# Two-layer decoder trunk on one core: GpSimd's two-operand steps given to VectorE, sigmoids computed by Tanh

## The chip, the core and the metric

One core of a Trainium2 chip runs the whole program. The metric is device microseconds of one execution. TensorE is PE in the profile, VectorE DVE, ScalarE ACT, GpSimd POOL, and SyncE SP, which only issues DMAs.

## The reference, cut to what matters

x is 1024 tokens by 1024 channels, mem 256 memory vectors. Each layer norms x, projects it, mixes it over time, adds a memory attention of 4 heads, gates with SiLU and projects back. Layer 0 mixes with 12 heads of causal attention whose queries and keys are built from normed low-rank projections and partly rotated; layer 1 with the recurrence of RWKV-7.

```python
for i in range(DEPTH):
    h, m = rmsnorm(x, norm_g[i]), rmsnorm(mem, mem_norm_g[i])
    mem_k, mem_v = split_cols(m @ w_mem_kv[i], (X_WIDTH, X_WIDTH))
    u = h @ (w_in_mla[0] if i == 0 else w_in_rwkv[0])
    # layer 1, of the columns of u:
    w = -jax.nn.softplus(-(w0 + jnp.tanh(wd) @ w2)) - 0.5
    decay = jnp.exp(-jnp.exp(w))
    a = jax.nn.sigmoid(a0 + ad @ a2)
    y = jnp.concatenate([mix, mem_out], axis=-1) * jax.nn.silu(gate)
    x = x + y @ w_out[i]
return rmsnorm(x, final_g)
```

The kernel computes exp(-exp(w)) as exp(-C0 * sigmoid(w0 + ...)) with C0 = exp(-0.5), and silu(gate) in layer 1 as gate * sigmoid(gate).

## The kernel before, in words

All matrices are kept transposed, channels on the 128 partitions and tokens along the row, in two halves (`hf`) of 512 tokens.

**Products by halves.** A product in fp32 is made of three in fp32r: each operand is split into a high half (ScalarE rounds it, `copy`) and a low half (the operand minus its high half). `mm3` (L162 to L164) issues high by high, low by high and high by low. `weights` (L142) does this for a weight tile of 128x512: a DMA into `wr`, ScalarE's cast to `wh` (L153), a subtraction to `wl` (L155). In layer 0 the subtraction is GpSimd's, with every second tile of the memory's weights (`shared`) on VectorE; `layer1` sets `lows`, and from there on all are VectorE's. `wr`, `wh` and `wl` have four buffers each, and a projection of 128 channels (`gemm`, 24 matmuls of 512 columns) uses two tiles. Two PSUM tiles (`mm`) take the products in turn.

**Norms.** `rstd` is a chain over three engines. ScalarE squares the tiles, VectorE adds them up (L186), TensorE sums over partitions (L208), VectorE takes an inverse square root by Newton steps on 8 elements per partition (L194 to L199) and widens it (L213), TensorE spreads it (L220), ScalarE copies it out (L222).

**Layer 0.** The opening loads x, splits it (`load_x`, L440 and L441), projects the first six blocks for both halves (`low`), norms them (`lora`), rotates the shared key (`rope`, whose second product L523 is GpSimd's), norms and splits the memory (`mem_load`, `mem_norm`: scale L255, halves L128 and L129) and projects it (`mem_kv`). Then come gates and memory heads, then attention, where each pair of heads is projected while earlier heads attend. There GpSimd makes the low halves of the rotated queries (L640, L641) and fills the masked corner of a tile with zeros (L730). The output projection follows.

**Layer 1.** 24 items (12 pairs of heads by 2 halves) pass through five stages that run side by side: `project`, `prep` (the decay and a by two sigmoids, L998, then exponentials, L1037 to L1040), `invert`, `scan`, `norm`. Gates (`gate`, L864) and memory heads (with the softmax exponential, L304) are strewn in. ScalarE evaluates a function from the table that is loaded; where the next function needs another, an ACT_TABLE_LOAD stands before it. Sigmoid and Exp are in different tables.

**What sets the order.** The code gives the program, but a scheduler reorders each engine's instructions when the program is built, by its own estimates of their durations and by the buffers. On the chip each engine takes its instructions strictly in that order, and so does SP's queue of DMAs. Moving a step to another engine thus moves others as well.

Of the kernel before, what the change touches and what calls it, by code (L numbers as in the profile page):

```python
# [13 lines left out]
F32 = mybir.dt.float32  # L14
# [3 lines left out]
AF = mybir.ActivationFunctionType  # L18
# [38 lines left out]
PNG, PMG, PFG, PQG, PKVG, PMU, PW0 = 0, 16, 32, 40, 43, 45, 82  # L57
# [14 lines left out]
class Build:  # L72
    def __init__(self, tc, A, st):
        self.tc, self.nc, self.A = tc, tc.nc, A
        self.n, self.lows = 0, False
        pool = lambda name, bufs, **kw: st.enter_context(tc.tile_pool(name=name, bufs=bufs, **kw))
        self.const = pool("const", 1)
        self.wp = pool("w", 4)
        self.w2p = pool("w2", 1)
        self.ws = pool("ws", 4)  # L80
        self.smp = pool("sm", 4)
        self.heap = pool("heap", 54)
        self.heap2 = pool("heap2", 12)
        self.mmp = pool("mmp", 2, space=PSUM)
        self.dram = pool("dram", 1, space=DRAM)
        self.ysp = [None, None]
        dt = lambda s: self.dram.tile([P, T], F32, tag=s, name=s)
        self.mkd = [[dt(f"mk{l}{i}") for i in range(2)] for l in range(2)]
        self.mvd = [[dt(f"mv{l}{i}") for i in range(2)] for l in range(2)]
        self.carry = [self.dram.tile([P, P], F32, tag=f"cr{p}", name=f"cr{p}") for p in range(NH)]  # L90
        self.setup()
# [31 lines left out]
        return self.prm[:, i : i + 1]  # L123


    def split(self, hi, lo, src):

        self.nc.scalar.copy(hi, src)  # L128
        self.nc.vector.tensor_sub(lo, src, hi.bitcast(F32))  # L129
# [9 lines left out]
        self.split(hi[:], lo[:], src)  # L139
        return hi, lo  # L140

    def weights(self, src, cols=1024, shared=False):  # L142


        nc = self.nc
        res = []
        for c in range(0, cols, T):
            n = min(T, cols - c)
            raw = self.wp.tile([P, T], F32, tag="wr", name=self.name("wr"))
            hi = self.ws.tile([P, T], F32R, tag="wh", name=self.name("wh"))  # L150
            lo = self.ws.tile([P, T], F32R, tag="wl", name=self.name("wl"))
            nc.sync.dma_start(raw[:, :n], src[:, c : c + n])
            nc.scalar.copy(hi[:, :n], raw[:, :n])  # L153
            sub = nc.vector.tensor_sub if self.lows or shared and len(res) % 2 else nc.gpsimd.tensor_sub
            sub(lo[:, :n], raw[:, :n], hi[:, :n].bitcast(F32))  # L155
            res.append((hi, lo))
        return res

# [104 lines left out]
    def mem_kv(self, l, ms):  # L263

        nc, A = self.nc, self.A
        mk, mv = [], []
        for h in range(4):
            if h % 2 == 0:
                mk.append(self.g([P, 2, 256], s="mk"))
            w = self.weights(A["wmk"][l, h], shared=True)  # L270
            ps = self.mmt()
            self.gemm(ps[:, :256], w, ms, 8)
            nc.scalar.copy(mk[-1][:, h % 2, :], ps[:, :256])
        for cb in range(2):
            ws = self.weights(A["wmv"][l, cb, 0], shared=True) + self.weights(A["wmv"][l, cb, 1], shared=True)
            ps = self.mmt()
            for mb in range(2):
                for k in range(8):
                    hi, lo = ws[k // 2]
                    o = (k % 2) * 256  # L280
                    m = tuple(x[:, mb * P : mb * P + P] for x in ms[k])
                    self.mm3(
                        ps[:, mb * 256 : mb * 256 + 256], m, (hi[:, o : o + 256], lo[:, o : o + 256]), k == 0, k == 7
                    )
            t = self.g(s="mv")
            nc.scalar.copy(t[:], ps[:])
            mv.append(t)
        for i, t in enumerate(mk):
            nc.sync.dma_start(self.mkd[l][i][:].rearrange("p (h m) -> p h m", h=2), t[:])
        for i, t in enumerate(mv):  # L290
            nc.sync.dma_start(self.mvd[l][i][:], t[:])
# [122 lines left out]
    def layer0(self, ahead):  # L414

        nc, A, tc = self.nc, self.A, self.tc
        with ExitStack() as st:
# [5 lines left out]
            b_tile = lambda: psb.tile([P, T], F32, tag="b", name=self.name("b"))  # L423
# [40 lines left out]
            raw = [[None] * 6 for _ in range(2)]  # L464
# [27 lines left out]
            cos, sin = tl([P, S], F32, "cos"), tl([P, S], F32, "sin")  # L492
# [23 lines left out]
            def rope(q, hf):  # L516

                sl = slice(hf * T, hf * T + T)
                sw, t = self.g(s="rs"), self.g(s="rt")
                for b in range(4):  # L520
                    nc.sync.dma_start(sw[32 * b : 32 * b + 32, :], q[32 * (b ^ 1) : 32 * (b ^ 1) + 32, :])
                nc.vector.tensor_mul(t[:], q[:], cos[:, sl])
                nc.gpsimd.tensor_mul(sw[:], sw[:], sin[:, sl])  # L523
                nc.vector.tensor_add(t[:], t[:], sw[:])
                return t

# [81 lines left out]
            def project(h):  # L608
# [26 lines left out]
                for t in rot:  # L635

                    a, b = self.g(dt=F32R, s="qsa"), self.g(dt=F32R, s="qsb")
                    nc.scalar.copy(a[0:64, :], t[0:64, :])
                    nc.scalar.copy(b[64:128, :], t[64:128, :])
                    nc.gpsimd.tensor_sub(a[64:128, :], t[0:64, :], a[0:64, :].bitcast(F32))  # L640
                    nc.gpsimd.tensor_sub(b[0:64, :], t[64:128, :], b[64:128, :].bitcast(F32))  # L641
                    hd["qr"].append(a)
                    heads[h + 1]["qr"].append(b)
                if h % 2 == 0:
# [134 lines left out]
    def layer1(self, x1, first, second):  # L779

        nc, A, tc = self.nc, self.A, self.tc
        with ExitStack() as st:
# [17 lines left out]
            nc.gpsimd.memset(rmask[:].rearrange("p (c t) -> p c t", t=64)[:, :, 0:1], 0.0)  # L800
            prev = tl([P, 37], F32, "prev")

            cen = tl([P, P], F32, "cen")
            nc.vector.scalar_tensor_tensor(cen[:], self.bones, -1.0 / 64, self.ident, ALU.mult, ALU.add)
            ARs = [tl([P, 8, 256], F32, f"AR{i}") for i in range(3)]
# [4 lines left out]

            self.ysp[1] = [[self.dram.tile([P, T], F32, tag=f"y1_{k}_{hf}", name=f"y1_{k}_{hf}") for hf in range(2)] for k in range(16)]
            am = self.cst[:, CAM : CAM + 256]
            env = dict(rmask=rmask, cen=cen, am=am, ip=ip, a_tile=a_tile, b_tile=b_tile, c_tile=c_tile, y_tile=y_tile)
            xns, twa = [None, None], [tl([P, T], F32R, f"twa{i}") for i in range(2)]
            items = [dict(AR=ARs[i % 3], XT=XTs[i % 2], U2=U2, p=i % NH, hf=i // NH, twa=twa) for i in range(2 * NH)]

# [44 lines left out]
            def gate(m, hf, tile=self.mmt):  # L861
                ps = proj(41 + m, hf, tile)
                sg = self.g(s="sg")
                nc.scalar.activation(sg[:], ps[:], AF.Sigmoid)  # L864
                nc.vector.tensor_mul(sg[:], ps[:], sg[:])
                return sg

# [70 lines left out]
                    next(gen, None)  # L938
                    yield

            self.lows = True
            N, now = 2 * NH, [0]
            stages = [(project, ST[0]), (lambda i: self.prep(items[i], env), ST[1]), (lambda i: self.invert(items[i], env), ST[2]), (scan, ST[3]), (norm, ST[4])]
            extra = {}
# [34 lines left out]
    def prep(self, d, env):  # L979
# [14 lines left out]
        for j, (t, bias) in enumerate(((sig, PW0), (a, PA0))):  # L994
            ps = a_tile()
            mm(ps[:], wh[:, j * P : j * P + P], twa[j][:], start=True, stop=False)
            mm(ps[:], wl[:, j * P : j * P + P], twa[j][:], start=False, stop=True)
            ACT.activation(t[:], ps[:], AF.Sigmoid, bias=self.pc(bias + p))  # L998

        yield  # L1000

# [377 lines left out]
```

## Time and profile before

| | us |
|---|---|
| three runs, median (lowest, highest) | 2541.62 (2540.92, 2550.03) |
| the profiled execution | 2544.33 |
| its span in the profile | 2542.6 |
| TensorE busy | 2434.1 |
| VectorE busy | 1883.6 |
| ScalarE busy | 1371.9 |
| GpSimd busy | 285.0 |

The span runs from the first to the last instruction; the rest of the execution's time lies around it. TensorE's busy time is no measure of its speed, since matmuls overlap and run at either of two clocks: 2.4 GHz, or half of it; PEclk is the mean share of the full clock in a stretch. Layer 0 takes the time up to about 1045 us.

### The profile page before, as it was taken

The numbers are of one execution on the slowest core, as the hardware profiler recorded it, in microseconds if no ns is written. First come the engines' busy times: TensorE is split into PE (matmuls) and PEld (weight loads), VectorE is DVE, ScalarE is ACT, GpSimd is POOL, SyncE is SP. The second block draws the span as 40 slices with busy tenths as digits, with TensorE's granted clock in tenths as the row PEclk, the third lists the DMA queues.
The fourth block names the chain that finished last, engine by engine and source line by source line (L and its number), as shares of the span: only waits on it lengthen the run. The fifth ranks groups of instructions, "written<-read, shape, count | busy, mean of one in ns | idle before, by whom it ended". The sixth has DMA issues, their size and how long they took to land.

```text
span 2542.6 us, 39928 instructions
## 1 busy us (share of the span) xinstructions
PE 2434.1 (96%) x13298; PEld 2003.9 (79%) x13298; DVE 1883.6 (74%) x5564; ACT 1371.9 (54%) x2971; POOL 285.0 (11%) x344
## 2 busy tenths in 40 slices
PE   7899999999999999999999999999999999999997
PEld 5688777888888787878777777877787777788885
DVE  6655433677777647679888888788888888786986
ACT  5444335555445434556566665666666665654542
POOL 3332222322222240000000000000000000000000
PEclk8899999999999999999999999999999999999998
DMA  4242222111111345331222222322222223232341
GB/s 155 88 157 96 91 83 80 50 50 60 55 54 56 135 140 178 122 106 61 80 67 70 74 83 82 120 76 76 69 78 74 75 80 102 92 105 97 115 141 69
DMA packets 165983, 231.46 MB, mean 91 GB/s; under 512 B 46096, under 2 KB 67984, under 8 KB 165776
## 3 DMA queue, kind: packets, MB, share of 16 engines
q1 hardware_dynamic: 165776, 228.90, 27.5%
q8 instruction: 105, 1.72, 0.3%
q14 instruction: 102, 0.84, 0.1%
HBM read 187.66 MB, written 37.49 MB: 89 GB/s over the span
## 4 chain that ended last, share of the span: by engine, by line
PE 69%; DVE 16%; ACT 6%; issue 3%; DMA 2%; SPq 0%; DVEq 0%; POOL 0%; ACTq 0%; POOLq 0%
PE mm L162 14%; PE mm L163 13%; PE mm L164 13%; PE a L1088 3%; DVE tmp L1139 2%; PE c L1221 2%; PE pt L726 2%; DVE U L1143 2%; PE c L1224 1%; PE po L162 1%; PE y L1228 1%; PE po L163 1%; DVE wl L155 1%; PE y L1227 1%; PE po L164 1%
## 5 line engine op out<-in xcount | busy, mean ns | idle before, releaser
L153 ACT CAST wh<-wr 128x512 fp32r<-128x512 f32 (+3 forms) x500 | 298.6, 599 | 461.6 <-PE mm L163 363.0
L162 PE MATMUL mm<-xnh,wh 128*128 128x512 f32 x912 | 374.1, 411 | 0.8 <-DVE qml L134 0.6
L163 PE MATMUL mm<-xnl,wh 128*128 128x512 f32 x912 | 371.4, 407 | 0.0
L164 PE MATMUL mm<-xnh,wl 128*128 128x512 f32 x912 | 369.8, 406 | 0.0
L155 DVE TENSOR_TENSOR wl<-wr,wh 128x512 fp32r<-128x512 f32 (+2 forms) x352 | 237.2, 676 | 98.7 <-ACT wh L153 79.8
L155 POOL TENSOR_TENSOR wl<-wr,wh 128x512 fp32r<-128x512 f32 (+1 forms) x148 | 186.3, 1263 | 579.4 <-ACT wh L153 446.0
L162 PE MATMUL mm<-yh,wh 128*128 128x512 f32 x492 | 199.8, 406 | 5.5 <-DVE xr L391 5.3
L164 PE MATMUL mm<-yh,wl 128*128 128x512 f32 x492 | 197.6, 402 | 0.0
L162 PEld LDWEIGHTS mm<-xnh,wh 128*128 128x128 f32 x912 | 172.2, 189 | 30.4 <-issue 2.6
L163 PE MATMUL mm<-yl,wh 128*128 128x512 f32 x492 | 196.1, 399 | 0.0
L163 PEld LDWEIGHTS mm<-xnl,wh 128*128 128x128 f32 x912 | 172.4, 189 | 27.2 <-issue 1.4
L164 PEld LDWEIGHTS mm<-xnh,wl 128*128 128x128 f32 x912 | 172.2, 189 | 27.2 <-issue 1.0
L1069 POOL MEMSET SAV<- 64x512 f32 x48 | 24.9, 524 | 1385.6 <-DVE m L1261 250.7
L162 PE MATMUL mm<-xh,wh 128*128 128x512 f32 x416 | 168.9, 406 | 7.2 <-ACT xh L440 7.2
L163 PE MATMUL mm<-xl,wh 128*128 128x512 f32 x416 | 168.6, 405 | 2.9 <-DVE xl L441 2.9
L164 PE MATMUL mm<-xh,wl 128*128 128x512 f32 x416 | 168.1, 404 | 0.0
L1139 DVE TENSOR_TENSOR tmp<-As,U 128x60 f32<-128x60 f32 (+24 forms) x744 | 156.8, 211 | 13.2 <-DMA U<-in_cst_dram 1.1
L1143 DVE TENSOR_TENSOR U<-U,tmp 128x60 f32<-128x60 f32 (+24 forms) x744 | 157.2, 211 | 11.9
L1235 ACT ACTIVATE sc<-S,f 128x128 f32<-128x128 f32 x168 | 67.4, 401 | 170.0 <-DVE S L1236 155.5
L304 ACT ACTIVATE p<-b,sm 128x512 f32<-128x512 f32 (+2 forms) x144 | 82.9, 579 | 117.2 <-DVE sm L301 78.0
L391 DVE TENSOR_TENSOR xr<-mm,xr 128x512 f32<-128x512 f32 x123 | 84.5, 689 | 77.7 <-PE mm L164 77.2
L162 PEld LDWEIGHTS mm<-yh,wh 128*128 128x128 f32 x492 | 93.1, 189 | 24.3 <-DVE xr L391 3.5
(362 smaller groups left out, 6214.3 us busy)
## 6 DMA issues: line engine op xcount, KB each, us to landing
wr<-in_wu_dram SPq DMA_DIRECT2D x292, 256.0 KB, 2.6
wr<-in_wo_dram SPq DMA_DIRECT2D x122, 256.0 KB, 2.6
yr<-y SPq DMA_DIRECT2D x60, 256.0 KB, 3.7
As<-sysd SPq DMA_DIRECT2D x24, 512.0 KB, 4.3
y<-y SPq DMA_DIRECT2D x32, 256.0 KB, 2.0
y<-sg SPq DMA_DIRECT2D x32, 256.0 KB, 2.0
g<-u SPq DMA_DIRECT2D x24, 256.0 KB, 2.4
gt<-g SPq DMA_DIRECT2D x24, 256.0 KB, 2.8
```

The source lines that it names most:

```text
L153: nc.scalar.copy(hi[:, :n], raw[:, :n])
L155: sub(lo[:, :n], raw[:, :n], hi[:, :n].bitcast(F32))
L162: mm(ps, a[0], b[0], start=start, stop=False)
L163: mm(ps, a[0], b[1], start=False, stop=False)
L164: mm(ps, a[1], b[0], start=False, stop=stop)
L304: nc.scalar.activation(p[:, :own], ps[:, :own], AF.Exp, bias=sm[:, 0:1], accum_out=sm[:, 2 + i : 3 + i])
L391: nc.vector.tensor_add(xs[m][:], ps[:], xs[m][:])
L726: nc.tensor.transpose(pt[:, o : o + P], src, self.ident)
L1088: mm(ps[:, j * 256 : j * 256 + 256], BK[c // 4][:, c % 4, :], AR[:, c, :], start=True, stop=True)
L1139: E.tensor_tensor(out=tmp[:, 0:u, 0:n], in0=As[:, 0:u, u : u + 1].broadcast_to([P, u, n]), in1=U[:, u : u + 1, i0:8].broadcast_to([P, u, n ...
L1143: E.tensor_tensor(out=U[:, 0:u, i0:8], in0=U[:, 0:u, i0:8], in1=tmp[:, 0:u, 0:n], op=ALU.add)
L1235: ACT.activation(sc[:], cur, AF.Copy, scale=fc)
```

## The change

`weights` no longer chooses: every subtraction is VectorE's. The second product of `rope` and the low halves of the rotated queries go to VectorE too. GpSimd keeps the fills (`memset`, `affine_select`). In layer 1 each Sigmoid becomes a Tanh of half the argument and a Copy with scale 0.5 and bias 0.5, in place; the biases of `prep` are halved once, at the layer's setup. Only 24 columns of parameters are scaled for that.

```diff
+    def sigmoid(self, out, src, bias=None):
+        ACT = self.nc.scalar
+        ACT.activation(out, src, AF.Tanh, scale=0.5, bias=0.0 if bias is None else bias)
+        ACT.activation(out, out, AF.Copy, scale=0.5, bias=0.5)
...
-    def weights(self, src, cols=1024, shared=False):
+    def weights(self, src, cols=1024):
...
-            sub = nc.vector.tensor_sub if self.lows or shared and len(res) % 2 else nc.gpsimd.tensor_sub
-            sub(lo[:, :n], raw[:, :n], hi[:, :n].bitcast(F32))
+            nc.vector.tensor_sub(lo[:, :n], raw[:, :n], hi[:, :n].bitcast(F32))
...
-                nc.gpsimd.tensor_mul(sw[:], sw[:], sin[:, sl])
+                nc.vector.tensor_mul(sw[:], sw[:], sin[:, sl])
...
-                    nc.gpsimd.tensor_sub(a[64:128, :], t[0:64, :], a[0:64, :].bitcast(F32))
-                    nc.gpsimd.tensor_sub(b[0:64, :], t[64:128, :], b[64:128, :].bitcast(F32))
+                    nc.vector.tensor_sub(a[64:128, :], t[0:64, :], a[0:64, :].bitcast(F32))
+                    nc.vector.tensor_sub(b[0:64, :], t[64:128, :], b[64:128, :].bitcast(F32))
...
+            half = self.prm[:, PW0 : PW0 + 24]
+            nc.vector.tensor_scalar_mul(half, half, 0.5)
...
-                nc.scalar.activation(sg[:], ps[:], AF.Sigmoid)
+                self.sigmoid(sg[:], ps[:])
...
-            ACT.activation(t[:], ps[:], AF.Sigmoid, bias=self.pc(bias + p))
+            self.sigmoid(t[:], ps[:], env["half"][:, bias - PW0 + p : bias - PW0 + p + 1])
```

The built order moves in two places of the opening. The lines of the changed kernel stand 4 or 5 further down (L212 is its L208, L224 its L220). On TensorE, around the sum of squares of the memory (`b_207`); `mm_234`, `mm_236`, `mm_244` and `mm_246` are four projections in this order, before first:

```order
L163 MATMUL mm_236_1157<-xl_90_513,wh_232_1125 128x512
L164 MATMUL mm_236_1157<-xh_89_512,wl_233_1126 128x512
L208 MATMUL b_207_1045<-cst_101,sqa_199_1022 128x2 x2
L162 MATMUL mm_236_1157<-xh_92_519,wh_232_1125 128x512
L163 MATMUL mm_236_1157<-xl_93_520,wh_232_1125 128x512
...
L163 MATMUL mm_244_1200<-xl_18_238,wh_239_1189 128x512
L220 MATMUL b_210_1063<-cst_101,rw_209_1061 128x128 x2
L164 MATMUL mm_244_1200<-xh_17_237,wl_240_1190 128x512
```

and of the change, down to the first matmuls that need the memory's tiles (`mh_213`, `ml_214`):

```order
L167 MATMUL mm_246_1227<-xl_65_412,wh_239_1189 128x512
L168 MATMUL mm_246_1227<-xh_64_411,wl_240_1190 128x512
L212 MATMUL b_207_1045<-cst_101,sqa_199_1022 128x2 x2
...
L224 MATMUL b_210_1063<-cst_101,rw_209_1061 128x128 x2
L168 MATMUL mm_246_1227<-xh_103_566,wl_243_1196 128x512
L166 MATMUL mm_246_1227<-xh_106_573,wh_242_1195 128x512
L167 MATMUL mm_246_1227<-xl_107_574,wh_242_1195 128x512
L168 MATMUL mm_246_1227<-xh_106_573,wl_243_1196 128x512
L166 MATMUL mm_255_1271<-mh_213_1071,wh_250_1260 128x256
L166 MATMUL mm_262_1309<-mh_213_1071,wh_257_1298 128x256
```

The sum now comes 39 matmuls later, with the rest of `mm_236`, all of `mm_244` and a quarter of `mm_246` ahead of it, and only four matmuls stand between the spread and the memory's first product, where 43 stood. On VectorE, around the end of the first half's squares (`sqa_31`) and the start of its square root (`n_40`), before:

```order
L186 TENSOR_TENSOR sqa_31_265<-sqa_31_265,sqb_37_282 128x512
L186 TENSOR_TENSOR sqa_31_265<-sqa_31_265,sqb_38_285 128x512
L210 TENSOR_SCALAR n_40_294<-b_39_289 128x8
L194 TENSOR_SCALAR n_40_294<-n_40_294 128x8
L195 TENSOR_SCALAR n_40_294<-n_40_294 128x8
```

and now:

```order
L190 TENSOR_TENSOR sqa_31_265<-sqa_31_265,sqb_37_282 128x512
L159 TENSOR_TENSOR wl_72_426<-wr_70_424,wh_71_425 128x512
L190 TENSOR_TENSOR sqa_31_265<-sqa_31_265,sqb_38_285 128x512
L159 TENSOR_TENSOR wl_83_474<-wr_81_472,wh_82_473 128x512
L214 TENSOR_SCALAR n_40_294<-b_39_289 128x8
L159 TENSOR_TENSOR wl_86_480<-wr_84_478,wh_85_479 128x512
L198 TENSOR_SCALAR n_40_294<-n_40_294 128x8
L199 TENSOR_SCALAR n_40_294<-n_40_294 128x8
```

Three low halves of weights, which were GpSimd's, now stand inside the chain of the norm.

## Rows read from the trace of the kernel before

**Rows 1.** The page's first part: each engine's busy us, share of the span, instructions.

```profile
span 2542.6 us, 39928 instructions
...
PE 2434.1 (96%) x13298; PEld 2003.9 (79%) x13298; DVE 1883.6 (74%) x5564; ACT 1371.9 (54%) x2971; POOL 285.0 (11%) x344
```

**Rows 2.** Table of stretches: us; PE, PEld, DVE, ACT, POOL busy (instructions); PEclk; DMA; GB/s.

```profile
0.00:160.00 160.00, 128.47 (x572) 103.70 (x573) 104.88 (x186) 72.58 (x129) 51.33 (x42) 0.91 0.37 123
...
500.00:860.00 360.00, 356.16 (x2269) 308.81 (x2268) 269.17 (x646) 186.84 (x469) 77.12 (x140) 1.00 0.18 57
...
1045.00:2500.00 1455.00, 1413.32 (x7804) 1149.29 (x7803) 1220.16 (x4164) 875.57 (x1911) 23.90 (x46) 1.00 0.27 87
```

**Rows 3.** Who TensorE waited for, 0 to 160 us: total us, times, longest us.

```profile
PE b L208 <- DVE sqa L186: 13.2, 4, 4.5
...
PE b L220 <- DVE rw L213: 4.3, 2, 3.1
...
PE mm L163 <- POOL wl L155: 1.1, 1, 1.1
```

**Rows 4.** Table of stretches again: after a wait, and the opening; PEclk before DMA share.

```profile
57.00:62.00 5.00, 4.83 (x15) 4.19 (x16) 2.13 (x13) 0.96 (x2) 0.27 (x1) 0.50 0.03 13
...
20.00:140.00 120.00, 102.44 (x426) 82.64 (x427) 82.63 (x156) 52.35 (x95) 37.58 (x26) 0.89 0.29 97
```

**Rows 5.** VectorE's groups, 0 to 160 us: busy us, mean ns, idle before.

```profile
L186 DVE TENSOR_TENSOR sqa<-sqa,sqb 128x512 f32<-128x512 f32 x17 | 18.1, 1063 | 1.1 <-ACT sqb L185 0.4
L441 DVE SCALAR_TENSOR_TENSOR xl<-x,prm,xh 128x512 fp32r<-128x512 f32 x16 | 15.9, 1024 | 7.4 <-ACT xh L440 7.4
L474 DVE TENSOR_TENSOR c<-c,rx 128x512 f32<-128x512 f32 x12 | 13.5, 1134 | 8.4 <-ACT c L473 4.8 <-ACT rx L222 3.6
```

**Rows 6.** The same view of the whole program: the low halves of weights on VectorE.

```profile
L155 DVE TENSOR_TENSOR wl<-wr,wh 128x512 fp32r<-128x512 f32 x334 | 231.5, 695 | 97.2 <-ACT wh L153 78.6 <-PE b L1151 9.8 <-PE c L1224 3.0
```

**Rows 7.** Timeline, 90 to 99 us: start us, us, engine and step.

```profile
90.08 5.06 POOL L155 TENSOR_TENSOR wl<-wr,wh 128x512 fp32r<-128x512 f32 x3 [6.39 <-ACT wh L153]
...
92.69 1.22 DVE L195 TENSOR_SCALAR n<-n 128x8 int32<-128x8 int32 x1
...
95.19 0.17 DVE L198 SCALAR_TENSOR_TENSOR n<-n 128x8 f32<-128x8 f32 x1
```

**Rows 8.** GpSimd's costliest group, whole program.

```profile
L155 POOL TENSOR_TENSOR wl<-wr,wh 128x512 fp32r<-128x512 f32 (+1 forms) x148 | 186.3, 1263 | 579.4 <-ACT wh L153 446.0 <-PE mm L164 37.6 <-DVE ptl L129 23.4
```

**Rows 9.** Timeline of TensorE, 22 to 29 us.

```profile
25.19 0.39 PE L163 MATMUL mm<-xl,wh 128*128 128x512 f32 x1
25.42 0.39 PE L164 MATMUL mm<-xh,wl 128*128 128x512 f32 x1
```

**Rows 10.** Timeline of VectorE, the memory's tiles: the first and last of four.

```profile
129.58 0.88 DVE L255 SCALAR_TENSOR_TENSOR mn<-memr,prm,rstd 128x256 f32<-128x256 f32 x2 [0.40 <-ACT rstd L222]
...
137.82 1.01 DVE L129 TENSOR_TENSOR ml<-mn,mh 128x512 fp32r<-128x512 f32 x1 [0.69 <-ACT mh L128]
```

**Rows 11.** ScalarE's groups, whole program.

```profile
L1010 ACT COPY sq<-n 128x512 f32<-128x512 f32 x24 | 14.8, 616 | 16.5 <-DVE n L199 16.5
...
L998 ACT ACT_TABLE_LOAD x22 | 28.2, 1283 | 0.4
```

**Rows 12.** Timeline of ScalarE, around one table load.

```profile
119.35 1.28 ACT L562 ACT_TABLE_LOAD   x1
120.65 0.63 ACT L562 ACTIVATE u<-u 128x512 f32<-128x512 f32 x1
```

**Rows 13.** Who TensorE waited for, 1045 to 2500 us.

```profile
PE y L1269 <- ACT yT L1244: 4.8, 19, 0.6
PE a L1077 <- ACT SAV L1072: 4.2, 12, 0.7
...
PE b L1151 <- ACT inv L1155: 3.6, 11, 0.4
PE a L336 <- ACT mp L304: 3.4, 7, 0.6
```

More of the change, by code (lines that the diff above doesn't have):

```diff
@@ L74, in __init__ @@
         self.tc, self.nc, self.A = tc, tc.nc, A
-        self.n, self.lows = 0, False
+        self.n = 0
         pool = lambda name, bufs, **kw: st.enter_context(tc.tile_pool(name=name, bufs=bufs, **kw))
@@ L269, in mem_kv @@
                 mk.append(self.g([P, 2, 256], s="mk"))
-            w = self.weights(A["wmk"][l, h], shared=True)
+            w = self.weights(A["wmk"][l, h])
             ps = self.mmt()
@@ L274, in mem_kv @@
         for cb in range(2):
-            ws = self.weights(A["wmv"][l, cb, 0], shared=True) + self.weights(A["wmv"][l, cb, 1], shared=True)
+            ws = self.weights(A["wmv"][l, cb, 0]) + self.weights(A["wmv"][l, cb, 1])
             ps = self.mmt()
@@ L812, in layer1 @@
             am = self.cst[:, CAM : CAM + 256]
-            env = dict(rmask=rmask, cen=cen, am=am, ip=ip, a_tile=a_tile, b_tile=b_tile, c_tile=c_tile, y_tile=y_tile)
+            env = dict(rmask=rmask, cen=cen, half=half, am=am, ip=ip, a_tile=a_tile, b_tile=b_tile, c_tile=c_tile, y_tile=y_tile)
             xns, twa = [None, None], [tl([P, T], F32R, f"twa{i}") for i in range(2)]
@@ L939, in part @@
                     yield
-            self.lows = True
             N, now = 2 * NH, [0]
```

## The prediction

> **What bounds the kernel now.** I read the page's first part, then the table of stretches, then who TensorE waited for, then the granted clock, then VectorE's and GpSimd's instructions one by one. TensorE is busy for 2434.1 of 2542.6 us [rows 1]. So at full clock only its holes, some 108 us, can be won, and what it loses at the lower clock. The table of stretches shows where the holes are [rows 2]: 31.5 us in the first 160 us, 3.8 us in the 360 us of attention from 500 on, 41.7 us in the 1455 us of the recurrent layer. The opening is by far the worst place, and there GpSimd and VectorE work at the same time.
>
> In the opening TensorE waits for the norms: 13.2 us in four waits at the row sums of squares (L208), 4.3 us at the spread of the result (L220), and once for GpSimd's low half of a weight tile, 1.1 us [rows 3], together 18.6 us. A wait costs twice. In the five us right after the wait that ends at 57.2 us the granted clock is 0.50, the lower of the two levels (1.2 instead of 2.4 GHz), and from 20 to 140 us it is 0.89 in the mean [rows 4]; the missing 0.11 of 120 us is 13.2 us of TensorE's work. What the opening has to give is at most 18.6 + 13.2 = 31.8 us.
>
> Why are the squares late? The sum of two tiles takes VectorE 1063 ns in the mean there, the low half of x 1024, the scaling by rx 1134 [rows 5], while the same kind of two-operand step over 128x512 takes 695 ns in the whole program [rows 6]. The timeline shows the reason: a step on 8 elements per partition took 1.22 us while GpSimd's subtractions ran from 90.08 to 95.14 us [rows 7]. The same sort of step takes 0.17 us as soon as GpSimd is done. VectorE stands still behind GpSimd. TensorE's order was fixed when the program was built, and such stops were evidently not in it: it put L208 where the squares should have been ready.
>
> **The change, part by part.**
>
> *GpSimd's steps in the opening.* GpSimd has 42 instructions in the first 160 us [rows 2]; six are the setting up, 36 go to VectorE. At 695 ns [rows 6] they add 36 x 0.695 = 25 us. What VectorE gets back, against 695 ns: 17 x 0.37 + 16 x 0.33 + 12 x 0.44 = 16.9 us from the three groups of [rows 5], and the stops of the small steps besides (1.05 us for the one in [rows 7]). So VectorE's 104.9 us stay near 110 of 160. GpSimd's own step took 1263 ns [rows 8], so a weight tile's low half is also ready 0.57 us sooner. The gain does not come from less work but from the order, which the two rows of the change show: the first norm's sums stand 3 matmuls later than before, the second 14, the third 17, the fourth 34, the memory's 39, counted in the built order. A matmul of 512 columns starts 0.23 us after the one before it at full clock [rows 9], so these are 0.7, 3.2, 3.9, 7.8 and 9.0 us of other work ahead of a wait whose longest was 4.5 us [rows 3]. With the squares no later than now, four of five waits are covered.
>
> What is late next: the memory's norm now ends only 4 matmuls before the first matmul that needs its normalized tiles. That chain (scale, high half, low half, four times over) ran from 129.58 to 138.83 us [rows 10], 9.2 us. Before, the rest of two tiles, 43 matmuls or 9.9 us, covered it. Now there are 4 x 0.23 = 0.9 us and, up to the last of the four tiles, 36 matmuls of half the width at half of 0.23, 4.1 us: a new wait of about 4.2 us, and up to 3 us of clock after it, as after the waits of today. With half a us left over at each of the five norms I lose 2.5 more. The opening: -31.8 + 4.2 + 3 + 2.5 = **-22 us**. Its ends are 0, if every wait comes back in another place, and -31.8.
>
> *The rest of the attention layer.* The fullest stretch is attention. Ten of the twelve heads are projected while it runs; that is 30 weight tiles, 10 rope products and 20 low halves of q, 60 steps at most, or 60 x 0.695 = 41 us on a VectorE that is busy for 269.2 of 360 us [rows 2], so 86% at most; what it gets back from stops lowers that. TensorE's 356.2 us are the cover, and its holes there are 3.8 us. The order on TensorE is reshuffled by 5 to 20 rows in this stretch. I take -2 us for shorter stops in the whole layer, between -4 and the price in the second rival.
>
> *The sigmoids.* Each becomes a Tanh and a Copy with scale and bias, in place. There are 24 x 2 in prep and 32 gates, so 80 more steps of ScalarE at 616 ns, the nearest row of a copy from and to SBUF [rows 11]: 49 us. In the built order the table loads go from 84 to 20, so that none is left in the recurrent layer; 64 x 1.283 [rows 11] = 82 us go. ScalarE, busy 875.6 of 1455 us in that layer [rows 2], is relieved by 33 us, 4%. A gate's PSUM tile is held one copy longer, but the load that stood ahead of 11 gates is gone. The one scaling of the biases takes 24 columns, once, at the start.
>
> A load stops ScalarE for 1.28 us and the next instruction starts 0.02 us after it [rows 12]. By the Trainium skill (ScalarE: Activation LUTs, "What ACT_TABLE_LOAD costs") a switch costs 1283 ns and another 1380 ns of drain, about 2.66 us. By that rule 64 switches would be 170 us and the relief 121 us; the trace shows the 1283 ns and no drain, and I go by the trace.
>
> What of the 33 us reaches TensorE? Its waits in this layer that ScalarE ends come to 16.0 us in four groups, of 0.4 to 0.7 us at the longest [rows 13]. A load of 1.28 us is longer than any of them, but most of these waits are for the copy that TensorE has just fed, with no load in front. Between 0 and 16.0 I take 4 us, a quarter, nearer to the share of 4% than to all.
>
> **The sum.** The profiled execution took 2544.3 us for a span of 2542.6. -22 - 2 - 4 = -28 gives 2516; the median of the three runs, 2541.6, lies 2.7 us below the profiled one, so I say **2515 us**.
>
> **The rivals.**
>
> *The waits come back* (chance 0.2). VectorE takes its instructions in order. In the new order the low halves of the next weights stand inside the norm: two between the sums and the square root's first step, one before its last. Each needs ScalarE's high half, and that needs a buffer that TensorE frees only after a whole block. If these hold the norm up for as long as the stops of GpSimd did, TensorE waits as before. For it: 25 us are added where 17 are surely given back. Against it: the order leaves 0.7 to 9 us more room. Then only -2 and -4 remain: 2536 to 2539 us, the same within 0.5%.
>
> *VectorE becomes the bound of the attention layer, and the kernel is slower* (0.1). At 86% and in order, a low half behind a softmax step comes too late for its matmul, which then waits 1.1 us, as it did for GpSimd's [rows 3]. 148 tiles move [rows 8]; if one in four brings such a wait, that is 37 x 1.1 = 41 us. From one in four on, 41 us outweigh the 28 by 0.5% (13 us); at one in three, with 54 us, it is 2568. Against it: VectorE still has 50 us free in this stretch, and does the step in half of GpSimd's time. The Trainium skill (Perfetto Trace Analysis, "Optimizing Scalar/DVE Operations") says that work may go to GpSimd when VectorE is saturated. By that rule, taking it back onto an engine at 86% is the wrong way; the same section adds that the two share a port, and rows 7 show that side of it.
>
> *ScalarE's relief counts in full* (0.1). If all four groups of [rows 13] go, the layer gives 16 and the sum is -40: 2502 us.
>
> That Tanh needs a load of its own, so that the change would not do what it says, is ruled out by the built order: after the last softmax of the first layer there is no load.
>
> **How the numbers follow.** The forecast has 0.6. The least that a measurement of this kernel can tell from no change is about 0.5%, 12.7 us: faster is below 2529, slower above 2554. Forecast and third rival lie below 2529, 0.7 together; the first rival between, 0.2; the second above, 0.1. The range goes from 2498, the opening's end of -31.8 with more than half of ScalarE's 16 us, up to 2545, past the first rival.
>
> **What would show it right or wrong.** In the changed profile GpSimd has nothing but fills; the groups of [rows 5] fall to about 700 ns; TensorE's waits at L208 in the first 160 us drop from 13.2 us to below 4 and the mean clock from 20 to 140 us rises above 0.95; a new wait of about 4 us stands at the memory's tiles; no ACT_TABLE_LOAD after the first layer; ScalarE's busy time falls by some 33 us; VectorE's share in attention stays below 86% and TensorE's holes there below 8 us. The forecast is wrong if the opening ends as late as before, or if TensorE waits for low halves of weights all through the first layer.

## The result, and the profile after

The changed kernel takes **2524.1 us** (median of 4 runs, 2519.6 to 2526.3), the kernel before 2541.3 on the same chip: a ratio of 0.9923, interval 0.9902 to 0.9943. A second set, beside other runs, gave 0.9920 (0.9906 to 0.9933). It is faster, by 17 us. The forecast was 2515 us, 9 us too low; the measured time lies inside its range. The section on right and wrong shows that two of its terms were off in opposite directions.

The profiled execution took 2523.6 us for a span of 2521.5. Page, first part:

```profile
span 2521.5 us, 39868 instructions
...
PE 2430.9 (96%) x13298; PEld 1998.7 (79%) x13298; DVE 1940.7 (77%) x5751; ACT 1335.0 (53%) x2987; POOL 55.3 (2%) x158
```

Against [rows 1]: GpSimd's busy time falls from 285.0 to 55.3 us (fills only), VectorE gains 57 us, ScalarE loses 37, TensorE's matmuls are the same 13298. The table of stretches, against [rows 2, 4] (columns as there):

```profile
0.00:160.00 160.00, 141.66 (x714) 116.78 (x715) 116.39 (x248) 84.81 (x149) 0.71 (x6) 0.99 0.45 147
20.00:140.00 120.00, 109.58 (x558) 90.83 (x557) 92.01 (x205) 62.46 (x113) 0.00 (x0) 0.99 0.38 124
...
500.00:860.00 360.00, 353.24 (x2229) 308.09 (x2228) 277.77 (x665) 180.96 (x445) 25.83 (x87) 1.00 0.21 69
1045.00:2500.00 1455.00, 1408.84 (x7732) 1137.48 (x7731) 1217.68 (x4156) 825.21 (x1913) 23.07 (x44) 1.00 0.26 86
```

In the first 160 us TensorE is busy for 13 us more, issues 714 matmuls instead of 572, and its clock from 20 to 140 us is 0.99 instead of 0.89. The other two stretches have slightly less TensorE time than before: by this table nothing is won there, though a stretch of fixed ends does not hold the same work in both kernels. VectorE's groups in the first 160 us, against [rows 5]:

```profile
L445 DVE SCALAR_TENSOR_TENSOR xl<-x,prm,xh 128x512 fp32r<-128x512 f32 x16 | 11.7, 749 | 2.0 <-ACT xh L444 1.9
L190 DVE TENSOR_TENSOR sqa<-sqa,sqb 128x512 f32<-128x512 f32 x17 | 11.7, 688 | 0.5
L478 DVE TENSOR_TENSOR c<-c,rx 128x512 f32<-128x512 f32 x12 | 8.2, 687 | 3.2 <-ACT rx L226 2.8 <-ACT c L477 0.4
```

The same steps on the same tiles take 749, 688 and 687 ns instead of 1024, 1063 and 1134. And TensorE's waits there, against [rows 3]:

```profile
PE mm L166 <- ACT xh L444: 7.3, 1, 7.3
PE mm L166 <- ACT mk L277: 3.2, 1, 3.2
PE b L212 <- DVE sqa L190: 2.3, 1, 2.3
PE mm L166 <- ACT mh L134: 1.6, 2, 1.1
PE b L224 <- DVE rw L217: 1.6, 2, 1.3
PE mm L167 <- DVE ml L135: 1.4, 4, 0.6
PE mm L167 <- DVE xl L445: 0.6, 2, 0.3
```

The first row is the start, which stands before as well. The waits for the norms' sums are down from 13.2 to 2.3 us and for the spread (now L224) from 4.3 to 1.6. The waits at the memory's tiles (`mh`, `ml`) are new, 3.0 us together, and so is one of 3.2 us for the copy of the memory's first keys.

A step of the program starts at another time in each kernel, and the difference is the lead so far. From the timelines, in us:

| step | before | changed | lead | moves alone (below) |
|---|---|---|---|---|
| memory's norm, first row sum | 122.7 | 106.6 | 16.1 | 106.4 |
| last copy of the memory's keys | 190.4 | 167.9 | 22.5 | 169.2 |
| attention, first product with the gate | 473.5 | 443.4 | 30.1 | 444.6 |
| attention, last such product | 872.7 | 843.4 | 29.3 | 844.5 |
| recurrent layer, preparation's 20th scan | 2092.8 | 2063.6 | 29.2 | 2062.4 |
| its 21st scan | 2150.6 | 2128.6 | 22.0 | 2120.3 |
| end of the span | 2542.6 | 2521.5 | 21.1 | 2517.9 |

So 22 us come in the opening, some 7 more by the end of attention, and 7 are lost again in one place late in the recurrent layer. Since the order differs, the work between two such steps can differ a little: from the 20th to the 21st scan TensorE has 313 matmuls in the changed kernel and 298 before. Counted by matmuls the loss is nearly the same: the 500 from the 11000th to the 11500th take 101.5 us instead of 95.2.

### The profile page after: what moved, and what is told of

The parts are those of the page before. It is cut to its first block, busy times and chain, and to the rows that moved or that the text cites. A ratio compares the mean times of both kernels' runs of the same rounds, so it can differ in the third digit from the quotient of the medians.

```text
span 2521.5 us, 39868 instructions
## 1 busy us (share of the span) xinstructions
PE 2430.9 (96%) x13298; PEld 1998.7 (79%) x13298; DVE 1940.7 (77%) x5751; ACT 1335.0 (53%) x2987; POOL 55.3 (2%) x158
## 4 chain that ended last, share of the span: by engine, by line
PE 76%; DVE 11%; ACT 7%; issue 2%; DMA 2%; SPq 0%; DVEq 0%; ACTq 0%
PE mm L166 16%; PE mm L167 15%; PE mm L168 15%; PE a L1093 3%; PE c L1226 2%; PE c L1229 2%; PE pt L730 2%; PE y L1233 1%; PE po L166 1%; PE po L167 1%; PE y L1232 1%; PE c L1220 1%; PE po L168 1%; PE c L1222 1%; DVE tmp L1144 1%
## 5 line engine op out<-in xcount | busy, mean ns | idle before, releaser
L159 DVE TENSOR_TENSOR wl<-wr,wh 128x512 fp32r<-128x512 f32 (+3 forms) x500 | 330.0, 661 | 135.9 <-ACT wh L158 116.5
L166 PEld LDWEIGHTS mm<-yh,wh 128*128 128x128 f32 x492 | 93.3, 190 | 23.0 <-DVE xr L395 3.5
L303 DVE TENSOR_REDUCE sm<-b 128x1 f32<-128x256 f32 (+1 forms) x176 | 90.3, 527 | 24.7 <-PE b L692 10.0
L168 PEld LDWEIGHTS mm<-yh,wl 128*128 128x128 f32 x492 | 93.0, 189 | 17.0 <-issue 0.2
```

The source lines that it names most:

```text
L159: nc.vector.tensor_sub(lo[:, :n], raw[:, :n], hi[:, :n].bitcast(F32))
L166: mm(ps, a[0], b[0], start=start, stop=False)
L168: mm(ps, a[1], b[0], start=False, stop=stop)
L303: nc.vector.tensor_reduce(sm[:, i : i + 1], ps[:, :own], AX.X, ALU.max, negate=True)
```

## The experiments

Each run was timed beside the kernel before. Ratios compare best, since the kernel before itself had medians of 2543.8, 2545.8 and 2545.3 us in the three sets.

### The two halves of the change

*e1_moves_only*, the change without the tanh:

```diff
-    self.sigmoid(sg[:], ps[:])
+    nc.scalar.activation(sg[:], ps[:], AF.Sigmoid)
```

(the preparation's sigmoids likewise, and the biases are not halved)

> All of GpSimd's two-operand steps go to VectorE, as in the change, but the recurrent layer keeps its Sigmoid. Against the kernel before, the changed kernel is 23 us ahead at the end of the memory's keys, 30 us ahead at the end of the attention layer, and only 21 us ahead at the end. Theory A: the moves give the 30 us and the tanh costs the 9 us that go in the recurrent layer, so this kernel ends near 2541 - 30 = 2511 us and keeps its lead of 30 us from the first layer's end to the last instruction. Theory B: the tanh gives the 4 us of the prediction and the 9 us are lost to something that the moves bring too, such as the clock at other places: then this ends at 2526 to 2530 us. Theory C: the tanh is worth nothing either way: 2524 us, as the changed kernel.

*e2_tanh_only*, the kernel before with `sigmoid` as in the change and GpSimd as it was.

> Only the sigmoids by the hyperbolic tangent; GpSimd keeps all its steps. Theory A (the tanh costs the 9 us that the changed kernel loses in the recurrent layer): 2541 + 9 = 2550 us. Theory B (the prediction's -4): 2537 us. Rival of the prediction (ScalarE's relief counts in full): 2541 - 16 = 2525 us. Theory C (nothing either way): 2541 us. In all of them ScalarE's busy time falls by some 33 us and no table load is left after the first layer.

Moves alone: 2518.5 us, **0.9900** (0.9887 to 0.9913). Tanh alone: 2556.5 us, **1.0051** (1.0036 to 1.0065). The two halves have opposite signs. The 2518.5 us lie between the figures of theories A and C, 2511 and 2524. The moves keep their lead of 30 us up to the 21st scan (last column of the table) and end 24.7 us ahead: some 3 us go between 2370 and 2390 us, where the clock is 0.83 in this execution. The runs e8 to e10 below have the same order of TensorE's matmuls and 1.00 at that place. The tanh alone has its loss where the changed kernel has it: its 20th scan starts at 2093.3 us, its 21st at 2157.8, 0.5 and 7.2 us behind the kernel before. It ends 12.2 us behind; some 5 of these go between 2410 and 2420 us, where its clock is 0.51. TensorE's waits around this place (2055 to 2135 us), in the changed kernel:

```profile
PE c L1226 <- ACT rk L1023: 1.3, 1, 1.3
PE a L1047 <- DVE f L1040: 1.1, 1, 1.1
PE a L1082 <- DVE BK L1063: 0.9, 1, 0.9
PE c L1220 <- DVE S L1241: 0.7, 1, 0.7
PE c L1226 <- DVE m L201: 0.7, 1, 0.7
PE c L1226 <- DVE gm L1224: 0.6, 2, 0.4
```

and with the moves alone, the same program but for the sigmoids:

```profile
PE c L1225 <- ACT rk L1022: 1.2, 1, 1.2
PE a L1046 <- DVE rk L1028: 1.1, 1, 1.1
PE c L1228 <- DVE SAV L1226: 0.8, 1, 0.8
```

The stretches show what stands behind the waits: first the changed kernel, then the moves alone.

```profile
2070.00:2080.00 10.00, 8.01 (x42) 6.62 (x41) 9.05 (x28) 6.47 (x14) 0.00 (x0) 0.83 0.29 103
2120.00:2130.00 10.00, 8.72 (x42) 7.29 (x41) 8.41 (x43) 3.97 (x7) 0.49 (x1) 0.84 0.21 74
```

```profile
2070.00:2080.00 10.00, 10.00 (x59) 8.48 (x58) 9.58 (x32) 6.34 (x13) 0.00 (x0) 1.00 0.48 159
2115.00:2125.00 10.00, 8.85 (x53) 7.49 (x51) 9.10 (x45) 5.40 (x9) 0.00 (x0) 1.00 0.16 48
```

After its waits the changed kernel gets a clock of 0.83 and 0.84 for ten us, the moves alone 1.00. That is 0.17 x 10 + 0.16 x 10 = 3.3 us, and the waits in the whole stretch are some 2.6 us more: most of the 7 us. The second set's profile of the changed kernel (*e12_change_again*) has both stretches of lower clock at the same places, so it is no accident of one execution. The lower clock is not needed for a loss here: e6 below, with the gates' tanh alone, has waits of this kind at a clock of 1.00.

> The changed kernel itself once more, on the same chip as the three others, to tell it from the moves alone (0.990 of the kernel before, interval 0.9887 to 0.9913). If the tanh costs: 0.9915 to 0.994, 2520 to 2527 us. If the two are the same: 0.990, 2518 us.

2524.8 us, 0.9920. The intervals of the change and of the moves alone touch (0.9906 to 0.9933, 0.9887 to 0.9913), so that these two runs alone would not settle that the tanh costs; the tanh alone, and the runs below, do.

### Where the moves gain

*e3_opening_only* switches the engine by stage: VectorE for all steps up to the memory's keys and values of both layers, GpSimd afterwards. *e4_rest_only* is the complement. Both keep the Sigmoid.

```diff
+            self.lows = False          # e4: True
             interleave((mem_heads(), 16), (early, 3), (lows(1), 9))
```

> Only the steps up to and with the memory's keys and values of both layers (the first 240 us, weights' low halves and the first rope product) go to VectorE; GpSimd keeps its steps from the memory heads on, and the Sigmoid stays. Theory A (the waits at the norms' sums and the lower clock behind them are the gain): the lead at the memory's keys is 23 us as in the changed kernel, it stays about the same afterwards, and the kernel ends at 2541 - 23 = 2518 us. Rival (the gain is spread over the whole layer, a bit at each step that VectorE no longer waits for): a lead of under 15 us at the memory's keys, and 2526 us or more.

> The complement: GpSimd keeps its steps in the first 240 us and loses all from the memory heads on (weights, rope products, low halves of the rotated queries); the Sigmoid stays. Theory A: no lead at the memory's keys, some 7 us by the first attention block, and 2541 - 7 = 2534 us. The prediction's own term for the rest of the layer was -2 us, that is 2539 us. Rival (VectorE becomes the bound in attention): slower than the kernel before, 2550 us or more.

The opening alone gives 0.9949 (0.9935 to 0.9962), 13 us; its lead at the memory's keys is 190.4 - 169.1 = 21.3 us, as foreseen, but it ends at 16.3 us in the profiled execution. The rest alone gives 0.9967 (0.9950 to 0.9985), 8 us; its lead at the first product of attention is 473.5 - 464.5 = 9.0 us. Neither is slower, so VectorE does not become the bound of attention. The two gains, 0.0051 + 0.0033, come near the 0.0100 of both.

### The stops or the order?

When GpSimd's steps move, the built order of all engines changes too. *e8_idle_gpsimd* takes the moves alone and lets GpSimd work for nothing in the opening:

```diff
+            if self.idle:
+                for o in (0, 128):
+                    nc.gpsimd.tensor_sub(self.spare[:, o : 384], raw[:, o : 384], hi[:, o : 384].bitcast(F32))
             res.append((hi, lo))
```

> The kernel with GpSimd's moves alone (2518.5 us), and for each of the 28 weight tiles of the first 130 us GpSimd also subtracts 640 columns into a tile that nobody reads. TensorE, VectorE, ScalarE and the DMA queue have exactly the order of the moves alone, so this brings back the stops of VectorE behind GpSimd without the old order. Theory A (the stops are the cause, the order only hid some of them): VectorE's sums of squares take 1.0 us again and the end of the memory's keys slips by 15 us or more: 2535 us. Theory B (the new order with its 0.7 to 9 us of room ahead of the norms is what gained, the stops are hidden by it): a slip of less than 6 us, 2524 us or less.

2550.7 us, **1.0016**: all the gain is gone, and more. But the idle steps also keep the weights' buffers from ScalarE (three high halves waited 4.7 us for GpSimd). *e10_idle_no_hold* was meant to remove that:

```diff
+            if self.idle:
+                nc.gpsimd.tensor_sub(self.spare[:, :8], raw[:, :8], hi[:, :8].bitcast(F32))
+                for o in (384, 128):
+                    nc.gpsimd.tensor_sub(self.spare[:, :o], self.spare[:, :o], self.spare[:, :o])
```

> As the run with idle subtractions in the opening (2550.7 us), but they read no buffer of a weight: per tile GpSimd takes 8 columns of the weight, as a clock, and then subtracts 512 columns of a tile of its own, 28 times, some 38 us against the 51 us of the kernel before; the order of the other engines is that of the moves alone. Theory A (VectorE's stops behind GpSimd are the cause by themselves): the end of the memory's keys slips by 10 to 20 us against the moves alone, 2530 to 2538 us. Theory B (the idle subtractions lost because they kept the weights' buffers from ScalarE's next high half): a slip under 5 us, 2524 us or less.

2533.7 us, **0.9955** (0.9942 to 0.9967). GpSimd was busy for 62.7 us in the first 160 us, more than the 38 meant, since it stops as well: its step on 8 columns took 521 ns in the mean, 1.83 us at the longest. The first copy of the memory's keys starts at 141.1 us, 14.0 us later than with the moves alone (127.1); in the kernel before it was 144.5. VectorE's groups in the first 160 us:

```profile
L194 DVE TENSOR_TENSOR sqa<-sqa,sqb 128x512 f32<-128x512 f32 x17 | 15.5, 910 | 0.5
L449 DVE SCALAR_TENSOR_TENSOR xl<-x,prm,xh 128x512 fp32r<-128x512 f32 x16 | 14.2, 903 | 1.4 <-ACT xh L448 1.2
L482 DVE TENSOR_TENSOR c<-c,rx 128x512 f32<-128x512 f32 x12 | 10.0, 837 | 4.9 <-ACT rx L230 2.8 <-ACT c L481 2.1
```

and TensorE's waits:

```profile
PE b L216 <- DVE sqa L194: 7.2, 4, 2.9
PE mm L170 <- ACT mk L281: 3.2, 1, 3.2
PE b L228 <- DVE rw L221: 3.1, 3, 2.0
PE mm L171 <- DVE xl L449: 2.2, 5, 1.1
```

The hold of the buffers did not go with it. ScalarE's own waits:

```profile
ACT wh L158 <- POOL spare L163: 8.2, 5, 2.5
...
ACT wh L158 <- POOL spare L161: 3.0, 2, 1.6
```

But TensorE waits for no half of a weight in this stretch, and VectorE's own time settles it. Up to the first copy of the keys, first the moves alone, then e10, then the kernel before (columns as in [rows 2]):

```profile
0.00:127.10 127.10, 109.12 (x486) 86.25 (x486) 91.62 (x204) 67.53 (x119) 0.71 (x6) 0.99 0.45 143
0.00:141.10 141.10, 114.61 (x486) 89.68 (x486) 106.97 (x204) 67.60 (x118) 62.74 (x91) 0.94 0.40 128
0.00:144.50 144.50, 116.84 (x486) 93.08 (x486) 93.19 (x169) 66.06 (x117) 46.76 (x38) 0.91 0.37 120
```

The same 204 steps take VectorE 15.4 us more in e10, and the copy slips by 14.0. In the kernel before, 169 steps took it longer than 204 do in the moves alone.

Every instruction of the other engines stands where it stands in the moves alone, and the data are the same. So the stops of VectorE behind GpSimd cost TensorE its waits by themselves, and the new order, with its room ahead of the norms, hides only a part of them.

*e9_idle_rest* has e8's idle steps beside the 77 weight tiles from the memory heads to the end of attention, and none in the opening.

> As the run with the idle subtractions in the opening, but here they stand beside the weight tiles from the memory heads to the end of attention (77 tiles), and not in the opening; the order of all other engines is again that of the moves alone. The rest of the first layer gave some 7 us in the changed kernel. Theory A (it gave them because VectorE no longer stops behind GpSimd): they go again, 2525 us, or more since these idle subtractions come on top of VectorE's own. Theory B (they came from the order): 2518 to 2520 us.

2533.2 us, 0.9945 (0.9928 to 0.9962): 0.0045 or 11 us are given back, again with the order unchanged (here the weights' buffers are held too, now from the DMA queue, so this is an upper end). In attention the softmax's scaling of a 128x512 tile shows it. Kernel before, moves alone, this run, 500 to 860 us:

```profile
L309 DVE TENSOR_SCALAR p<-p,sm 128x512 f32<-128x512 f32 x64 | 41.1, 655 | 1.7
```

```profile
L313 DVE TENSOR_SCALAR p<-p,sm 128x512 f32<-128x512 f32 x59 | 30.6, 534 | 1.6
```

```profile
L316 DVE TENSOR_SCALAR p<-p,sm 128x512 f32<-128x512 f32 x60 | 34.7, 592 | 1.6
```

### What the tanh costs

Three runs on the moves alone. *e6_gates_tanh* has the tanh in the 32 gates only, *e7_prep_tanh* in the preparation's 48 only. *e5_no_loads_no_copies* has neither loads nor copies:

```diff
-    nc.scalar.activation(sg[:], ps[:], AF.Sigmoid)
+    nc.scalar.activation(sg[:], ps[:], AF.Exp, scale=0.0)
```

> The kernel with GpSimd's moves alone (2518.5 us), and in place of each Sigmoid an exponential with scale 0: its output is a constant where the reference has the sigmoid (the decay, the a gate and the output gate are therefore other numbers), but ScalarE has neither the 64 table loads nor the 80 copies, so some 82 us less work in the recurrent layer. Theory A (the cost of the tanh is the cost of any new order of this layer, ScalarE's time itself is worth next to nothing): 2512 to 2524 us, and TensorE's waits for ScalarE do not shrink by more than 3 us. Theory B (ScalarE's time counts, the tanh lost because its copies lengthen the chain of the gates and of the preparation): 2505 us or less, as the four groups of waits for ScalarE, 16 us in the kernel before, go.

> The kernel with GpSimd's moves alone (2518.5 us), with the 32 gates by the hyperbolic tangent and the 48 sigmoids of the preparation left as they were. If the loss of the changed kernel against the moves alone (2524 against 2518.5) comes from the gates' longer hold of their PSUM tile (one copy more, and the wait of 1.1 us of TensorE for the gate's product), it stands here too: 2522 to 2526 us, with that wait. If it comes from the preparation's chain, this ends at 2518 us without the cluster of waits that the changed kernel has from 2063 to 2076 us. If any new order of the layer costs some us, it is anywhere from 2514 to 2530 us with waits at other places.

> The kernel with GpSimd's moves alone (2518.5 us), with the 48 sigmoids of the preparation by the hyperbolic tangent and the 32 gates left with the Sigmoid; the complement of the run with the gates alone (2526 us). Theory A (the cost is the gates' chain, one copy more between a gate's matmuls and the release of its PSUM tile): 2516 to 2520 us here. Theory B (the new order of the recurrent layer loses some us with any change of ScalarE's work that keeps VectorE as full as it is): 2522 to 2528 us, with waits of TensorE for VectorE around the preparation's steps near 2060 to 2130 us.

The last, *e11_tanh_folded*, starts from the change and folds the affine step of the gates and of `a` into VectorE's products and the column scales:

```diff
-                self.sigmoid(sg[:], ps[:])
-                nc.vector.tensor_mul(sg[:], ps[:], sg[:])
+                nc.scalar.activation(sg[:], ps[:], AF.Tanh, scale=0.5)
+                nc.vector.scalar_tensor_tensor(sg[:], sg[:], 1.0, ps[:], ALU.add, ALU.mult)
...
-        V.tensor_mul(a[:], a[:], kk[:])
+        V.scalar_tensor_tensor(a[:], a[:], 1.0, kk[:], ALU.add, ALU.mult)
```

> The changed kernel with 56 of its 80 copies folded away: a gate is (tanh + 1) times its sum in one VectorE step, the a gate's half and one are folded into the steps that use it, and the halves into the layer's column scales; no table load and 24 copies are left, so ScalarE has some 67 us less work than with the Sigmoid. The run with neither loads nor copies took 2511.6 us. If it is the copies in the gates' and the preparation's chains that cost: 2510 to 2514 us, the fastest of all. If any new order of the layer costs some us: 2518 to 2526 us.

| kernel | loads after the first layer | copies: gates, preparation | ScalarE busy, 1045 to 2500 us | us | ratio (interval) |
|---|---|---|---|---|---|
| moves alone | 66 | 0, 0 | 864.1 | 2518.5 | 0.9900 (0.9887 to 0.9913) |
| e7, preparation | 58 | 0, 48 | 881.6 | 2521.7 | 0.9906 (0.9893 to 0.9920) |
| e6, gates | 48 | 32, 0 | 853.7 | 2526.2 | 0.9921 (0.9905 to 0.9937) |
| the change | 0 | 32, 48 | 825.2 | 2524.8 | 0.9920 (0.9906 to 0.9933) |
| e11, folded | 0 | 0, 24 | 793.2 | **2512.3** | 0.9873 (0.9858 to 0.9888) |
| e5, neither | 0 | 0, 0 | 783.3 | 2511.6 | 0.9865 (0.9848 to 0.9883) |

Of these runs e6 and e11 came out as the first of their alternatives has it. e7 lies between the ranges of its two theories, and e5 just below A's and well above B's.

ScalarE's busy time does not order the times: the change has 39 us less of it than the moves alone and is slower. The gates' 32 copies do: both kernels with them stand at 0.992, both without loads and without them at 0.987. From the change to e11, with no load in either, 56 copies fewer (32 of the gates, 24 of `a`) give 0.0047, 12 us, with intervals well apart. The preparation's copies cost nothing that can be told (0.9906 against 0.9900), but the intervals leave room for some us, and e6's overlaps e7's. So the times alone do not put the cost on the gates. The traces add this, for the 500 matmuls from the 11000th to the 11500th: the kernels with the gates' copies take 101.5 and 101.7 us (the change, twice), 100.0 (the tanh alone) and 97.6 (e6); the seven with the Sigmoid 95.2 to 95.5; e7 94.5, e5 93.4, e11 93.3. Without the gates' copies, taking the loads away is worth 7 to 9 us by the ratios (e11, e5 against the moves alone; the intervals of e11 and the moves alone just touch).

e11 keeps the computation and beats both kernels, 1.27% under the kernel before. Its row of TensorE's stretch, beside the changed kernel's above: TensorE does as much there with less from ScalarE.

```profile
1045.00:2500.00 1455.00, 1410.44 (x7760) 1138.92 (x7758) 1219.33 (x4174) 793.19 (x1861) 23.15 (x44) 1.00 0.28 86
```

What stays open: whether a gate's copy costs through its own chain (the PSUM tile is held for one copy more; TensorE waits once, 1.1 us, for a gate's product in the change and in the tanh alone, 1.0 in e6, 0.5 in e7) or through the order that the builder makes around it. The waits near 2070 us name VectorE's `f` and `BK`, not a gate, which speaks for the order. No run has the copies in an unchanged order.

## Why the prediction was right or wrong

**The bound and the place: right.** The opening was the worst place, and both halves of its price were there: TensorE's waits at the norms' sums and spreads fell from 17.5 to 3.9 us, and the clock from 20 to 140 us rose from 0.89 to 0.99 (0.96 in e12). But the 31.8 us were no upper bound. The sum left out TensorE's other waits for VectorE, 5.4 us in the kernel before, of which 0.6 is left:

```profile
PE mm L163 <- DVE xl L441: 2.9, 4, 0.8
PE mm L164 <- DVE wl L155: 1.5, 2, 1.0
...
PE mm L163 <- DVE wl L155: 1.0, 1, 1.0
```

**The opening, -22: right in size, measured 22.5, in part by luck, and its reason was half wrong.** The text said that the gain comes from the order and not from less work. With the new order and GpSimd busy again (e10) 14.0 of the 17.4 us that the moves gain up to the first copy of the keys are lost. So the stops themselves were most of the cost. The other 3.4 us may be the order's; the split is rough, since GpSimd's load and VectorE's are not those of the kernel before. "With the squares no later than now, four of five waits are covered" fell: in e10 four of the five sums start no later than before (27.2, 56.9, 74.9 and 122.2 us against 28.2, 57.2, 75.4 and 122.7), and TensorE waits at each of the four, 7.2 us together instead of 13.2. The luck is that the 4.8 us gained outside the sum come to about as much as two losses it did not foresee, a wait of 3.2 us (next paragraph) and 1.4 us more at the norms than the 2.5 put down for them. Every sign held: the groups are at 690 to 750 ns, the L208 wait at 2.3 us (below 4), the clock above 0.95.

**The wait at the memory's tiles, 4.2 plus 3 of clock: near.** It is 3.0 us in six waits, and no lower clock follows it. A wait of 3.2 us that was not forecast comes behind it, and has the lower clock. ScalarE's row shows why:

```profile
125.59 0.65 ACT L277 COPY mk<-mm 128x256 f32<-128x256 f32 x2 [2.23 <-DVE ang L501]
```

and VectorE's what that waited for:

```profile
125.08 0.43 DVE L501 CAST ang<-pos 128x512 f32<-128x512 int32 x1 [1.00 <-DMA pos<-in_pos_dram]
```

The copy of the first keys wants a buffer that is free once VectorE has read the positions, and their DMA landed late. This comes with the new order and not with the early opening: in e10, where the same copy stands 14.0 us later, TensorE waits 3.2 us for it too, and in the kernel before, which is later still, 0.2.

**The rest of the first layer, -2: mis-sized, it is -7.** From the last copy of the keys to the last product of attention the lead grows from 22.5 to 29.3 us. Up to the first product of attention the change takes 275.5 us instead of 283.1, with 1364 matmuls instead of 1379. In the kernel before TensorE waited 4.2 us in this stretch, 2.5 of them for a softmax's scaling, 0.9 us at a time; in the changed one 0.6. I had looked only at attention proper, from 500 us on, where TensorE had few holes; it takes 399.2 us before and 400.0 in the change, which has the 15 matmuls there. VectorE's share there is 77%, below the 86% of the bound, and TensorE's holes 6.8 us, below 8.

**The sigmoids, -4: wrong in sign.** The step that failed is "Between 0 and 16.0 I take 4 us". The sum of ScalarE's work was right: 80 copies took 50.2 us (forecast 49), the loads are gone, its busy time fell by 37 (forecast 33). But the range ended at 0, and no lower end was given for a longer chain and another order. The runs put the term at some +5 us on top of the moves (0.9920 against 0.9900, intervals that touch) and at +13 alone, of which some 5 are the lower clock near 2415 us. A relief was there to be had, 7 to 9 us without the gates' copies; with them it is gone and some 5 us besides. Nor does it come by the waits that were counted for it: in e5 TensorE's waits for ScalarE between 1045 and 2500 us are 22.6 us, in the moves alone 20.4.

**The sum: inside the range by errors that cancel.** In the profile the terms came to -22.5, -6.8 and, for all that follows attention, +8.2, together the lead of 21.1 us; the forecast had -22, -2 and -4. Of the 8.2 the moves alone lose 3.5 as well, in part to the lower clock after 2370 us, which no term held.

**The rivals.** *The waits come back* did not happen, and *VectorE becomes the bound* did not (e4 is faster). Beside that rival stood the Trainium skill (Perfetto Trace Analysis, "Optimizing Scalar/DVE Operations"), by which moving work to GpSimd may make sense when VectorE is saturated. At 77% VectorE is not, and taking the work back gave 8 us (e4), while GpSimd's work beside it cost 11 us (e9). *ScalarE's relief in full*, 16 us, is not reached even with all 66 loads of 1.283 us, 85 us, gone and no copy added (e5: 7 to 9 us against the moves alone). The case that did come, a gain in the first layer and a loss in the recurrent one, was none of them.

## What to carry to other kernels

Before GpSimd is given a two-operand step to relieve VectorE, look at the mean time of VectorE's own steps in that stretch: where equal steps took half as long again, as here, the relief was a cost, and it landed on whoever waits for VectorE's chain. Replacing a function to save table loads pays when its affine rest folds into an operation that is there anyway; as an instruction of its own it can cost more than the loads, and which of the two it is shows in the time of the layer, not in ScalarE's busy time. When a tuned program is built in a new order, a term of a few us needs an end on both sides.

## What was not expected of the hardware

The stop works both ways. In e10 a step of GpSimd on 8 columns took 0.21 us while VectorE was on steps of 8 columns itself, and 1.83 us seven us later:

```profile
86.56 0.21 POOL L161 TENSOR_TENSOR spare<-wr,wh 128x8 f32<-128x8 f32 x1 [1.17 <-issue]
...
93.20 1.83 POOL L161 TENSOR_TENSOR spare<-wr,wh 128x8 f32<-128x8 f32 x1 [5.03 <-issue]
```

During the second VectorE had three low halves and a sum of squares without a gap, and GpSimd's step ended as the last of them did, at 95.0 us:

```profile
92.48 1.89 DVE L135 TENSOR_TENSOR cl<-c,ch 128x512 fp32r<-128x512 f32 x3
94.28 0.69 DVE L194 TENSOR_TENSOR sqa<-sqa,sqb 128x512 f32<-128x512 f32 x1
```

And TensorE's lower clock does not follow every wait: 1.2 us for `rk` near 2117 us in the moves alone left the ten us around it at 1.00, nearly the same wait (1.3 us) in the changed kernel left 0.84. What TensorE had done before differs there, in the changed kernel a cluster of waits stands some 50 us ahead. But the same work does not settle it either. At 2371 us in the moves alone and at 2391 us in e10 TensorE waits 1.4 and 1.5 us for the same `X`, in the same order of instructions. The stretches behind, first the moves alone, then e10:

```profile
2375.00:2380.00 5.00, 5.00 (x21) 4.57 (x20) 1.61 (x9) 1.35 (x3) 0.00 (x0) 0.51 0.50 160
2395.00:2405.00 10.00, 10.00 (x61) 8.28 (x62) 9.23 (x52) 2.96 (x7) 0.00 (x0) 1.00 0.45 151
```

What decides was not tried.
